# A decoder layer on one core: one more reserved k-block at the product boundaries, turned blocks in two PSUM banks, a longer written order and a shorter norm chain

## The chip, the cores and the metric

The kernel runs on one core of a Trainium2 chip. The core has a matrix engine (TensorE, "PE" in the profile, with its weight loads as "PEld"), a vector engine (VectorE, "DVE"), a scalar engine (ScalarE, "ACT"), GpSimd ("POOL"), SyncE ("SP", which here issues the loads) and 16 DMA engines. Each engine works through its own queue of instructions in order and waits for the others by semaphores. SBUF holds operands, and PSUM holds what TensorE accumulates: here eight banks of 128 x 512 fp32. The metric is device time in microseconds (us), the median of the runs.

## The reference: one decoder layer in fp32

The input x is 256 tokens of 2048 numbers. A vector c gives, through a matrix w_ada, nine vectors of 2048 (three shifts, three scales, three gates):

```python
mod = (c_act @ w_ada[l] + b_ada[l]).reshape(b, N_MOD, D_MODEL)
h = modulate(rms_norm(x, norm_ffn1[l]), mod[:, 0], mod[:, 1])
x = x + 0.5 * mod[:, 2][:, None, :] * swiglu(h, w_ffn1_gu[l], w_ffn1_down[l])
h = modulate(rms_norm(x, norm_mix[l]), mod[:, 3], mod[:, 4])
x = x + mod[:, 5][:, None, :] * token_mixing(h, w_in[l], w_ret_branch[l], w_swa_branch[l], w_out[l], sinks[l])
h = modulate(rms_norm(x, norm_ffn2[l]), mod[:, 6], mod[:, 7])
x = x + 0.5 * mod[:, 8][:, None, :] * swiglu(h, w_ffn2_gu[l], w_ffn2_down[l])
return rms_norm(x, norm_final)
```

`swiglu(h, w_gu, w_down)` splits `h @ w_gu` into a gate and an up half of 5632 columns each and returns `(silu(gate) * up) @ w_down`. `token_mixing` is one product with `w_in`, a retention and a sliding-window attention, and a product with `w_out`. `rms_norm` divides a token's row by the root of the mean of its squares (plus 1e-6); `modulate` is `h * (1 + scale) + shift`. Three times, then, a product ends that writes into x (here called the down product: 5632 to 2048, 2048 to 2048, 5632 to 2048), a norm over the whole row of x follows, and twice the next product starts from the normed row. These places are the boundaries.

## The kernel before

**Products.** The 256 tokens are two halves t = 0, 1 of 128. An fp32 product is made of three products in a reduced format, fp32r: each operand is split into a high part (ACT's cast) and the rest (DVE's subtraction), and `products()` (L342 to L344) issues high x high, low x high and high x low for each half and each 128 rows of the sum ("k-tile"). A weight chunk is 512 rows (one "k-block") by 512 columns, loaded by SP into one of four `raw` buffers; it is split in two half-blocks of 256 rows (cast `wh` L350, subtraction `wl` L352), with three buffers each for high and low. A half-block for both halves of the tokens is 12 matmuls. Activations that lie in a `slot` are split in pairs (`Whole.pair`, L385 and L386) into two "a" buffers; those of a normed row are kept whole, split, in `Held` ("hh", "hl").

**PSUM.** Four banks accumulate products ("pa"), two hold turned blocks ("ps"), and two ("pd") serve for smaller things, the unread output of the squares among them.

**Order.** A scheduler orders PE, DVE and ACT freely, with one exception each for a down product's end and the norm behind it, which stand inside `manual_schedule(engines=ORDERED)` and so in the order in which the code is written. SP is always in written order. In `down_product`, two column chunks (0 and 1) come first, with free order. Of the second pair of chunks (2 and 3), the last three k-blocks are reserved: chunk 2 is computed there for both halves, chunk 3 is only split, into buffers that are kept (`late`, `home`), and then computed half by half: `last(0, steps)` for t = 0 in one go, and for t = 1 in six steps of six matmuls, handed on as `tail`. In this way the first half's row of x is complete while TensorE still has six steps to do. `add_gated` (L571, L572) multiplies a bank with the gate and adds it to x, and ACT sums the squares (L487).

**The norm and the next product's head** (`into_norm`). `inv_rms` (L499 to L513) adds the four chunks' squares, takes a root on ACT and a reciprocal with one Newton step on DVE. Of each half, four blocks of 512 columns are then scaled (`normed`, L533), turned by four transposes into one PSUM bank (`turned`, L540), scaled and shifted by columns (`modulated4`: the first two, once three, columns on ACT, L552, and the others on DVE, L554) and split into `Held` (`to_held`, L563 and L564). The first chunk of the next product (its "head", two banks) is computed as the blocks come. The first boundary leads from the first feed-forward's down product to `w_in`, the second from `w_out` to the second feed-forward, and the third to the output (`final`, from L1220).

**The conditioning.** The nine vectors are worked out on DVE beside the products, paced by `set_pace` and `tick` over a given number of half-blocks.

## Time and profile before

| | |
|---|---|
| median of 3 runs | 2422.79 us (2422.41 to 2423.88) |
| the profiled execution | 2424.86 us |
| its span, from first to last instruction | 2423.1 us |
| granted TensorE clock | 0.999 |
| busy: PE, PEld | 2376.9 us (98%), 1936.8 us (80%) |
| busy: DVE, ACT, POOL | 1700.1 us (70%), 1290.0 us (53%), 5.6 us (0%) |
| read from HBM | 595.06 MB, 246 GB/s over the span |

A row of a timeline gives the start in us from the span's start, the duration, engine, line, operation, out<-in by the program's names, shape, how many stand in a row, and in brackets the idle time ahead and whose work ended it. A row of busy windows gives the stretch and its length, then busy us and count of PE, PEld, DVE, ACT and POOL, then granted clock, DMA share and GB/s. A row of groups gives line, engine, operation, shapes and count, then busy us and mean ns of one, then the idle time ahead and whom it waited for. A row of waits gives who waits for whom, the idle time in us, how often, and the longest. The first boundary lies at about 742 to 802 us of the span, the second at about 1653 to 1713, the last reserved section at about 2383 to 2393 with the output behind it.

### The profile page before, as it was taken

Reading aid. Unit: us, or ns where it says so; the run is one execution under the profiler, and the core shown is the slowest. Engines: PE = TensorE matmul, PEld = TensorE weight load, DVE = VectorE, ACT = ScalarE, POOL = GpSimd, SP = SyncE. Lnnn points to the kernel's source line nnn. Section 1 sums busy time; section 2 is a strip of 40 time slices with the busy share of each in tenths; the row PEclk is TensorE's granted clock in tenths of the full one; section 3 lists DMA queues with packets and bytes.
Section 4 is the critical chain, followed back from the end, with each engine's and each line's share of the span. In section 5 each row is a group of like instructions: output and inputs, shape, how many; then the busy total and the mean of one; then the engine's idle time right before and its main releaser. Section 6 shows DMA issues by size and latency. Waiting matters only on the chain. (4 is left out here: it accounts for less than half of the span.)

```text
span 2423.1 us, 28959 instructions
## 1 busy us (share of the span) xinstructions
PE 2376.9 (98%) x10678; PEld 1936.8 (80%) x10678; DVE 1700.1 (70%) x2736; ACT 1290.0 (53%) x1789; POOL 5.6 (0%) x14
## 2 busy tenths in 40 slices
PE   7999999999999999999999999999999999999998
PEld 4778888888787787778888788887888888888886
DVE  6998887778877668876766776767655555545656
ACT  6544544454545456665555554455555545454544
POOL 0000000000000000000000000000000000000000
PEclk9999999999999999999999999999999999999999
DMA  9997689998875697766679887765677887875563
GB/s 351 337 333 286 215 312 307 372 311 307 302 270 191 243 270 224 226 232 213 212 257 288 252 281 263 278 199 183 224 245 234 244 253 242 257 225 191 185 200 122
DMA packets 307184, 614.29 MB, mean 254 GB/s; under 512 B 72737, under 2 KB 73121, under 8 KB 288225
## 3 DMA queue, kind: packets, MB, share of 16 engines
q1 hardware_dynamic: 305538, 605.78, 75.0%
q0 software_dynamic: 928, 5.61, 0.7%
q8 instruction: 84, 1.38, 0.2%
q10 hardware_dynamic: 576, 1.05, 0.1%
q14 instruction: 58, 0.48, 0.1%
HBM read 595.06 MB, written 2.12 MB: 246 GB/s over the span
## 5 line engine op out<-in xcount | busy, mean ns | idle before, releaser
L352 DVE TENSOR_TENSOR wl<-raw,wh 128x1024 fp32r<-128x1024 f32 (+1 forms) x828 | 994.0, 1208 | 557.1 <-ACT wh L350 552.3
L350 ACT CAST wh<-raw 128x1024 fp32r<-128x1024 f32 (+1 forms) x828 | 859.7, 1041 | 960.7 <-PE pa L343 940.4
L342 PE MATMUL pa<-wh,hh 128*128 128x512 f32 x2224 | 870.3, 392 | 3.4 <-ACT wh L350 2.8
L343 PE MATMUL pa<-wh,hl 128*128 128x512 f32 x2224 | 869.0, 391 | 2.2 <-DVE hl L528 1.8
L344 PE MATMUL pa<-wl,hh 128*128 128x512 f32 x2224 | 796.7, 392 | 4.1 <-DVE wl L352 3.7
L344 PEld LDWEIGHTS pa<-wl,hh 128*128 128x128 f32 x2224 | 415.1, 188 | 97.4 <-DVE wl L352 10.4
L342 PEld LDWEIGHTS pa<-wh,hh 128*128 128x128 f32 x2224 | 418.1, 188 | 93.4 <-ACT wh L350 4.2
L343 PEld LDWEIGHTS pa<-wh,hl 128*128 128x128 f32 x2224 | 418.3, 188 | 91.8 <-issue 3.0
L343 PE MATMUL pa<-wh,a 128*128 128x512 f32 x992 | 384.0, 389 | 1.4 <-DVE a L386 1.4
L344 PE MATMUL pa<-wl,a 128*128 128x512 f32 x992 | 366.7, 390 | 2.2 <-DVE wl L352 2.2
L342 PE MATMUL pa<-wh,a 128*128 128x512 f32 x992 | 367.3, 390 | 1.2 <-DVE t L571 1.2
L344 PEld LDWEIGHTS pa<-wl,a 128*128 128x128 f32 x992 | 185.9, 188 | 42.7 <-DVE wl L352 4.5
L342 PEld LDWEIGHTS pa<-wh,a 128*128 128x128 f32 x992 | 186.1, 188 | 41.2 <-DVE t L571 1.9
L343 PEld LDWEIGHTS pa<-wh,a 128*128 128x128 f32 x992 | 186.2, 188 | 40.5 <-DVE a L386 2.2
L206 DVE CUSTOM_DVE_ANT_0 slot<-slot,cact 128x512 f32<-128x512 f32 (+1 forms) x252 | 193.0, 815 | 30.2 <-DMA slot<-in_w_ada_dram 30.0
L206 DVE CUSTOM_DVE_ANT_0 raw<-raw,cact 128x512 f32<-128x512 f32 (+1 forms) x260 | 167.3, 696 | 49.3 <-DMA raw<-in_w_ada_dram 39.1
L386 DVE TENSOR_TENSOR a<-slot,a 128x512 fp32r<-128x512 f32 x124 | 84.9, 685 | 13.6 <-ACT a L385 13.6
L385 ACT CAST a<-slot 128x512 fp32r<-128x512 f32 x124 | 76.4, 618 | 14.8 <-PE pa L344 14.7
L467 ACT COPY slot<-back 128x512 uint16<-128x512 uint16 x116 | 77.2, 767 | 0.0
L453 ACT COPY flat<-t 128x512 uint16<-128x512 uint16 x104 | 59.1, 619 | 4.1 <-DVE t L1097 3.8
L206 DVE DVE_READ_ACCUMULATOR2_ANT sums<- 128x1 f32 x512 | 42.4, 83 | 0.0
L487 ACT ACTIVATE pd<-x_sb 128x512 f32<-128x512 f32 x32 | 19.0, 593 | 34.8 <-DVE x_sb L572 32.5
(166 smaller groups left out, 990.2 us busy)
## 6 DMA issues: line engine op xcount, KB each, us to landing
raw<-in_w_ffn_gu_dram SPq DMA_DIRECT2D x152, 1024.0 KB, 5.5
raw<-in_w_in_dram SPq DMA_DIRECT2D x104, 1024.0 KB, 5.3
raw<-in_w_ffn_down_dram SPq DMA_DIRECT2D x88, 1024.0 KB, 5.2
slot<-in_w_ada_dram SPq DMA_DIRECT2D x76, 1024.0 KB, 7.5
raw<-in_w_ada_dram SPq DMA_DIRECT2D x64, 1024.0 KB, 5.2
raw<-in_w_ffn_gu_dram SPq DMA_DIRECT2D x24, 768.0 KB, 6.9
raw<-in_w_swa_branch_dram SPq DMA_DIRECT2D x16, 1024.0 KB, 5.6
raw<-in_w_ret_branch_dram SPq DMA_DIRECT2D x16, 1024.0 KB, 5.2
```

The lines of the kernel that those rows point to most:

```text
L206: nc.vector.tensor_tensor_reduce(out=w[:, at], in0=w[:, at], in1=cact[:, at], scale=1.0, scalar=0.0, op0=ALU.mult, op1=ALU.add, accum_out= ...
L342: nc.tensor.matmul(ps, ah[:, j, ts], wh[:, j, :], start=first, stop=False)
L343: nc.tensor.matmul(ps, al[:, j, ts], wh[:, j, :], start=False, stop=False)
L344: nc.tensor.matmul(ps, ah[:, j, ts], wl[:, j, :], start=False, stop=last)
L350: cast.append(nc.scalar.copy(hi, src).ins)
L352: nc.vector.tensor_sub(lo, src, hi.bitcast(F32))
L385: nc.scalar.copy(hi, v)
L386: nc.vector.tensor_sub(lo, v, hi.bitcast(F32))
L453: nc.scalar.copy(planes[:, i, :], words(src)[:, :, i])
L467: nc.scalar.copy(into[:, :, :, i], held["turned"][:, i])
L487: nc.scalar.activation(side_bank(), src, AF.Square, accum_out=dest)
```

## The change

Seven edits, all at the boundaries and the norms:

1. The last four instead of the last three k-blocks are reserved, so `tail` has eight steps of six matmuls. The first of the four keeps its activation pairs in buffers of its own ("back"), and its weights of chunk 3 in the half of the next `Held` that is not yet written (`spare_of`; at the program's end in a tile of the freed "hl").
2. A turned block lies in two banks: ACT's columns in "ps", DVE's in "pd". `ON_ACT` says how many columns are ACT's (2 or 3 of 4).
3. The order is written as a list of words. A digit pair is the half and the block: n norm, t transposes, ma and md the columns of ACT and DVE, h and l the split, p six matmuls of the head (half, k-block, half-block); tail0 to tail7 are six matmuls each; w10a and w10d the high and low part of half-block 0 of the head's weight 1; mul, add, sq the gated addition in pieces; rs, v, q, r the norm chain.
4. The list ends with the first weights of the product that follows the head (x0a to x1d), handed on as `ahead`; their load stands with the head's.
5. The norm chain: squares of three chunks are added beforehand (`mean_of_three`), and when the fourth is there, ACT takes `Abs_reciprocal_sqrt` and DVE makes the Newton step in two operations beside one that is independent of the root; the factor -1/2 that this leaves goes into the scalings (`HALF`), and where there is none, into one more small multiplication at the kernel's start.
6. The unread output of the last square goes to an SBUF tile ("flat") and the normed blocks too.
7. The first conditioning stretch is paced over 150 instead of 154 half-blocks.

```diff
-    def gemm_part(act, w, col0s, banks, kb, KT):
+    def gemm_part(act, w, col0s, banks, kb, KT, ahead=None):
...
-            raw = load(w, kb, c0)
+            raw = None if ahead else load(w, kb, c0)
...
-                wh, wl = split(wsp, "w", raw[:, 2 * h : 2 * h + 2, :], CH)
+                if ahead:
+                    wh, wl = ahead[h]
+                else:
+                    wh, wl = split(wsp, "w", raw[:, 2 * h : 2 * h + 2, :], CH)
...
+    def weight_by_parts(w, kb, c0, home=None):
+        raw = load(w, kb, c0)
+        made = {}
+        def high(h):
+            if home is None:
+                made[h] = [
+                    wsp.tile([P, 2, CH], F32R, tag=tag, name=nm(tag)) for tag in ("wh", "wl")
+                ]
+            else:
+                views = home()
+                made[h] = [view[:, 2 * h : 2 * h + 2, :] for view in views]
+            nc.scalar.copy(made[h][0], raw[:, 2 * h : 2 * h + 2, :])
+        def low(h):
+            hi, lo = made[h]
+            pace["behind"] = nc.vector.tensor_sub(
+                lo, raw[:, 2 * h : 2 * h + 2, :], hi.bitcast(F32)
+            )
+        return high, low, made
...
-    def square_sum(dest, src):
-        nc.scalar.activation(side_bank(), src, AF.Square, accum_out=dest)
+    def flat_tile():
+
...
-        nc.scalar.activation(r, s, AF.Sqrt, bias=eps, scale=1.0 / D)
...
+    HALF = -0.5
+    class Root:
+        def __init__(self, ssq, t):
+            self.base = mean_of_three(ssq, t)
+            self.last = ssq[:, t * 4 + 3 : t * 4 + 4]
+            self.r, self.v, self.q = (small(1, tag) for tag in ("rs1", "var", "rq1"))
+        def root(self):
+            nc.scalar.activation(
+                self.r, self.last, AF.Abs_reciprocal_sqrt, bias=self.base, scale=1.0 / D
+            )
+        def mean(self):
+            nc.vector.tensor_scalar(
+                out=self.v, in0=self.last, scalar1=1.0 / D, scalar2=self.base,
+                op0=ALU.mult, op1=ALU.add,
+            )
+        def near(self):
+            nc.vector.scalar_tensor_tensor(
+                out=self.q, in0=self.v, scalar=self.r, in1=self.r, op0=ALU.mult, op1=ALU.mult
+            )
+        def nearer(self):
+            nc.vector.scalar_tensor_tensor(
+                out=self.r, in0=self.q, scalar=-3.0, in1=self.r, op0=ALU.add, op1=ALU.mult
+            )
...
-        for kb in range(nb - 3):
+        for kb in range(nb - 4):
...
+            def place(kb, h):
+                if kb >= a:
+                    halves = home[:, (kb - a) * 2 + h].rearrange("p (i n) -> p i n", i=2)
+                    return [halves[:, i] for i in range(2)]
+                if kb == a - 1:
+                    return None
+                return [back.tile([P, CH], F32R, tag="back", name=nm("back")) for _ in range(2)]
+            for kb in (a - 2, a - 1, a, b):
...
-                n = kb + 1 if kb < b else a - 1
-                wt = weight(w, n, c0s[1], None if n < a else home_tile())
+                n = {a - 2: a - 2, a - 1: a, a: b, b: a - 1}[kb]
+                wt = weight(
+                    w, n, c0s[1], spare if n == a - 2 else None if n < a else home_views()
+                )
                 late[n] = [(n, h, wt(h)) for h in range(2)]
-            steps = [step for kb in (a - 1, a, b) for step in late[kb]]
+            steps = [step for kb in (a - 2, a, a - 1, b) for step in late[kb]]
...
+            def gated(t):
+                y[t] = t512()
+                nc.vector.tensor_mul(y[t], banks[1][t], gate[:, c0 : c0 + CH])
+            def added(t):
+                xs = x_sb[:, t, c0 : c0 + CH]
+                nc.vector.tensor_add(xs, xs, y[t])
+            def squared(t):
+                square_sum(
+                    ssq[:, t * 4 + 3 : t * 4 + 4], x_sb[:, t, c0 : c0 + CH], flat_tile
+                )
             after(
-                ssq,
-                lambda t: add_gated(banks[1][t], t, c0s[1], gate, ssq),
-                [lambda i=i: last(1, steps[i : i + 1]) for i in range(6)],
-            )
...
+    ORDER = """
+            w10a tail0 mul0 add0 tail1 sq0 rs0 v0 tail2 q0 r0 n00 n02 t00 tail3 md00
+            ma00 n03 h00 tail4 n01 w20a l00 t02 w21a w20d tail5 ma02 md02 w10d t01 tail6
+            h02 w21d w11a p000 ma01 l02 md01 tail7 w11d h01 t03 w30a mul1 p020 l01 w31a
...
+    ON_ACT = (2, 3, 3, 3, 2, 3, 3, 3)
...
+            wide = {"w1": weight_by_parts(w, 1, c0)}
+            wide["w2"] = weight_by_parts(w, 2, c0, at_first_use(home_views))
+            wide["w3"] = weight_by_parts(w, 3, c0, at_first_use(home_views))
+            wide["x"] = weight_by_parts(w, 0, c1)
+            xn, hs, ps = {}, {}, {}
+            def norm(t, kb):
+                xn[t, kb] = flat_tile()
+                xs = x_sb[:, t, kb * CH : (kb + 1) * CH]
+                nc.vector.tensor_scalar(
+                    out=xn[t, kb], in0=xs, scalar1=roots[t].r, scalar2=HALF,
+                    op0=ALU.mult, op1=ALU.mult,
+                )
+            def turn(t, kb):
+                ps[t, kb] = bank(), side_bank()
+                for j in range(KB):
+                    js = slice(j * P, (j + 1) * P)
+                    to = ps[t, kb][j >= ON_ACT[t * 4 + kb]]
+                    nc.tensor.transpose(to[:, js], xn[t, kb][:, js], ident)
...
+            def high(t, kb):
+                h4, hi, _ = of_held(t, kb)
+                nc.scalar.copy(hi, h4)
+            def low(t, kb):
+                h4, hi, lo = of_held(t, kb)
+                nc.vector.tensor_sub(lo, h4, hi.bitcast(F32))
...
+            for word in ORDER:
+                name = word.rstrip("0123456789")
+                if word[0] in "wx":
+                    of, h, low_part = word[:-2], int(word[-2]), word[-1] == "d"
+                    wide[of][low_part](h)
+                    if low_part and of != "x":
+                        parts[int(of[1]), h] = wide[of][2][h]
+                elif name in whole:
+                    whole[name](int(word[len(name) :]))
+                else:
+                    block[name](*map(int, word[len(name) :]))
+            ahead.update(wide["x"][2])
...
-    set_pace([(2, None, 0.5), (4, 1, None), (3, None, None)], 154, place, AQ)
+    set_pace([(2, None, 0.5), (4, 1, None), (3, None, None)], 150, place, AQ)
...
-    held, head, *calls = into_norm(3, wi, O_SK)
-    down_product(Whole(tiles), dn, gate, KF, *calls)
+    held, head, ahead, *calls = into_norm(3, wi, O_SK, O_SV)
+    down_product(Whole(tiles), dn, gate, KF, spare_of(held), *calls)
...
-    b = in_chunk(O_SV)
+    b = gemm(held, wi, [O_SV], ahead=ahead)[0]
```

How this moves instructions, at three places of DVE's queue. The first is the first boundary, from the first half's first scaling (out is the scaled block, `rs` the root) over the columns (`modc` scale and shift) and the splits (`hl`, `wl`, `home` are low parts), before:

```order
L533 TENSOR_SCALAR t_5920<-x_sb,rs_1048_5911 128x512 [waits DVE_49]
L533 TENSOR_SCALAR t_5922<-x_sb,rs_1048_5911 128x512
L352 TENSOR_TENSOR wl_5965<-raw_5896,wh_5964 128x1024 [waits PE_49,Activation_49]
L554 TENSOR_SCALAR t_5968<-ps_5948,modc 128x128 [waits PE_49,Activation_49]
L554 TENSOR_SCALAR t_5968<-ps_5948,modc 128x128
L564 TENSOR_TENSOR hl_4137<-t_5968,hh_4136 128x4x128 [waits Activation_49]
L533 TENSOR_SCALAR t_5975<-x_sb,rs_1048_5911 128x512
L533 TENSOR_SCALAR t_5977<-x_sb,rs_1048_5911 128x512
L554 TENSOR_SCALAR t_5979<-ps_5959,modc 128x128 [waits PE_49,Activation_49]
L571 TENSOR_TENSOR t_5995<-pa_5057,row_2516 128x512 [waits PE_49]
```

and with the change:

```order
L791 TENSOR_SCALAR flat_5932<-x_sb,rs_1039_5885 128x512 [waits DVE_49]
L791 TENSOR_SCALAR flat_5934<-x_sb,rs_1039_5885 128x512
L819 TENSOR_SCALAR t_5948<-pd_5937,modc 128x128 [waits PE_49]
L819 TENSOR_SCALAR t_5948<-pd_5937,modc 128x128
L791 TENSOR_SCALAR flat_5953<-x_sb,rs_1039_5885 128x512
L791 TENSOR_SCALAR flat_5962<-x_sb,rs_1039_5885 128x512 [waits DVE_49]
L835 TENSOR_TENSOR hl_4141<-t_5948,hh_4140 128x4x128 [waits Activation_49]
L467 TENSOR_TENSOR home_5964<-raw_5896,home_5964 128x1024 [waits DMAHW7_49,Activation_49]
L819 TENSOR_SCALAR t_5981<-pd_5968,modc 128x128 [waits PE_49]
L467 TENSOR_TENSOR wl_5903<-raw_5894,wh_5902 128x1024 [waits DMAHW6_49]
```

The columns' rows (L554, now L819) named a wait for PE and ACT and now name PE alone, from a "pd" bank; the weights' subtractions (L467) stand further back among the blocks.

The second place is the second boundary's down product, the first reserved k-block of chunks 2 and 3 with the gated additions of chunks 0 and 1 (`row` is the gate, `raw` the weight, `slot` the activations), before:

```order
L352 TENSOR_TENSOR wl_12922<-raw_12919,wh_12921 128x1024
L386 TENSOR_TENSOR a_12913<-slot_10598,a_12913 128x512
L571 TENSOR_TENSOR t_12889<-pa_12579,row_10597 128x512
L571 TENSOR_TENSOR t_12894<-pa_12580,row_10597 128x512
L352 TENSOR_TENSOR wl_12938<-raw_12919,wh_12937 128x1024
L572 TENSOR_TENSOR x_sb<-x_sb,t_12889 128x512
L572 TENSOR_TENSOR x_sb<-x_sb,t_12894 128x512
```

and with the change:

```order
L385 TENSOR_TENSOR back_12937<-slot_10596,back_12936 128x512
L603 TENSOR_TENSOR t_12887<-pa_12577,row_10595 128x512
L603 TENSOR_TENSOR t_12892<-pa_12578,row_10595 128x512
L352 TENSOR_TENSOR wl_12941<-raw_12914,wh_12940 128x1024
L604 TENSOR_TENSOR x_sb<-x_sb,t_12887 128x512
L604 TENSOR_TENSOR x_sb<-x_sb,t_12892 128x512
L445 TENSOR_TENSOR hl_12575<-raw_12956,hh_12574 128x1024
L603 TENSOR_TENSOR t_12897<-pa_12579,row_10595 128x512
L603 TENSOR_TENSOR t_12902<-pa_12580,row_10595 128x512
L445 TENSOR_TENSOR hl_12575<-raw_12956,hh_12574 128x1024
L385 TENSOR_TENSOR a_12964<-slot_10596,a_12964 128x512
L352 TENSOR_TENSOR wl_12968<-raw_12962,wh_12967 128x1024
```

The additions begin at the same place, ahead of `wl_12941`, the k-block's second weight; the two subtractions into `hl` (chunk 3's weight of this k-block) come among them, and six of the eight half additions (L603, L604) precede `wl_12968`, the next k-block's first weight.

The third place is the program's end, from the last gated multiplication to the last root, before:

```order
L571 TENSOR_TENSOR t_18442<-pa_17583,row_13494 128x512
L572 TENSOR_TENSOR x_sb<-x_sb,t_18442 128x512
L1226 TENSOR_TENSOR t_18438<-x_sb,gf 128x512
L499 TENSOR_REDUCE sum_18448<-ssq_16737 128x1
L503 TENSOR_SCALAR var_18449<-sum_18448 128x1
L506 RECIPROCAL rs_3273_18450<-rs_3273_18450 128x1
L507 SCALAR_TENSOR_TENSOR rq_3274_18451<-var_18449,rs_3273_18450 128x1
L510 TENSOR_SCALAR rq_3274_18451<-rq_3274_18451 128x1
L513 TENSOR_TENSOR rs_3273_18450<-rs_3273_18450,rq_3274_18451 128x1
```

and with the change:

```order
L739 TENSOR_TENSOR t_18442<-pa_17580,row_13500 128x512
L743 TENSOR_TENSOR x_sb<-x_sb,t_18442 128x512
L1313 TENSOR_TENSOR t_18438<-x_sb,gf 128x512
L565 TENSOR_SCALAR var_18360<-ssq_16734,base_18356 128x1
L571 SCALAR_TENSOR_TENSOR rq_3260_18361<-var_18360,rs_3258_18359 128x1
L576 SCALAR_TENSOR_TENSOR rs_3258_18359<-rq_3260_18361,rs_3258_18359 128x1
```

Six operations between the last addition and the scaling have become three.

More of the change, by code (lines that the diff above doesn't have):

```diff
@@ L664, in down_product @@
                 for h in range(2):
[L665 to L668 removed]
+                    pairs[kb].append(act.pair(kb * 2 + h, place(kb, h)))
                     products(
@@ L784, in layer_kernel @@
+        return held, banks, ahead, before, after
     gu, dn = w_ffn1_gu[0], w_ffn1_down[0]
@@ L844, in layer_kernel @@
             )
-    r = [inv_rms(ssq, t) for t in range(NT)]
+    r = [Root(ssq, t).all() for t in range(NT)]
+    for t in range(NT):
+        nc.vector.tensor_scalar(out=r[t], in0=r[t], scalar1=HALF, scalar2=None, op0=ALU.mult)
     bounds = (0, 2, 5, 8, 12, 16)
@@ L1234, in final @@
             scaled(3)
-            r = inv_rms(ssq, t)
+            r = roots[t].all()
             for ci in range(4):
```

253 lines of the change are left out of this document (109 added, 144 removed).

## The prediction

> **What bounds the kernel now.** I read the page's busy times first, then TensorE's matmuls in the timeline, then its busy time around the three reserved stretches, then who it waited for there.
>
> ```profile
> PE 2376.9 (98%) x10678; PEld 1936.8 (80%) x10678; DVE 1700.1 (70%) x2736; ACT 1290.0 (53%) x1789; POOL 5.6 (0%) x14
> ...
> 745.31 0.51 PE L344 MATMUL pa<-wl,home 128*128 128x512 f32 x1 [0.64 <-DVE wl L352]
> 746.12 0.39 PE L344 MATMUL pa<-wl,home 128*128 128x512 f32 x1
> 750.66 0.39 PE L343 MATMUL pa<-wh,home 128*128 128x512 f32 x1
> ...
> 742.00:802.00 60.00, 55.06 (x246) 42.32 (x245) 46.74 (x82) 34.30 (x58) 0.53 (x1) 1.00 0.53 182
> 1653.00:1713.00 60.00, 56.00 (x251) 43.46 (x250) 46.27 (x79) 35.85 (x60) 0.00 (x0) 1.00 0.48 164
> 2383.00:2393.00 10.00, 9.29 (x38) 6.78 (x37) 10.00 (x12) 8.64 (x11) 0.00 (x0) 1.00 0.59 210
> ...
> 742.00:802.00 60.00, 4.88 (x32) 3.82 (x32) 1.00 0.53 182
> ```
>
> TensorE is the bound and works almost always, so a time can only come out of what it loses. From 746.12 to 750.66 stand 20 matmuls: 0.227 us each when nothing is missing, though each shows 0.39 (they overlap). Busy time therefore hides losses, and I count matmuls. The windows give span, then PE, PEld, DVE and ACT busy with counts; the last row is the transposes alone (L540, 32 of them, 8 groups of 4).
>
> First boundary: 246 - 32 = 214 wide matmuls x 0.227 = 48.6 us. A group of transposes takes 0.44 us undisturbed (769.83 to the next matmul below, 0.35, plus 0.09 of restart): 3.5 us. 60.0 - 48.6 - 3.5 = 7.9; the count takes in the matmuls cut at both ends, so up to 0.4 more. I take 8.2 us. Second: 219 x 0.227 = 49.7, so 6.8 to 7.2; I take 7.1. Last reserved section: 10.0 - 38 x 0.227 = 1.4 to 1.8; I take 1.6. **16.9 us** in all is lost around these stretches; that is the most the change can win on TensorE there. Who is waited for, at the first one (idle alone, without restarts):
>
> ```profile
> PE ps L540 <- DVE t L533: 1.4, 2, 1.0
> PE pa L344 <- DVE wl L352: 1.3, 3, 0.6
> PE pa L342 <- ACT wh L350: 1.2, 1, 1.2
> PE pa L342 <- ACT hh L563: 0.5, 1, 0.5
> PE pa L343 <- DVE hl L564: 0.5, 2, 0.2
> ```
>
> Two kinds, then: the turned blocks and splits of the handover, and at the section's start the split weights (745.31 above). The handover in detail, from the end of the last product's first half:
>
> ```profile
> 764.58 0.69 DVE L571 TENSOR_TENSOR t<-pa,row 128x512 f32<-128x512 f32 x1 [0.93 <-PE pa L344]
> 766.63 0.19 ACT L487 ACTIVATION_READ_ACCUMULATOR pd<-x_sb 128x1 f32 x1
> 766.85 0.16 DVE L499 TENSOR_REDUCE sum<-ssq 128x1 f32<-128x4 f32 x1 [0.85 <-ACT pd L487]
> 767.04 0.30 ACT L502 ACTIVATE rs<-sum,eps 128x1 f32<-128x1 f32 x1 [0.22 <-DVE sum L499]
> 767.57 0.22 DVE L507 SCALAR_TENSOR_TENSOR rq<-var,rs 128x1 f32<-128x1 f32 x1
> 768.21 0.88 DVE L533 TENSOR_SCALAR t<-x_sb,rs 128x512 f32<-128x512 f32 x2
> 769.83 0.60 PE L540 MATMUL ps<-small_c,t 128*128 128x128 f32 x4
> 770.46 0.81 ACT L552 ACTIVATE t<-ps,modc 128x128 f32<-128x128 f32 x2 [2.19 <-PE ps L540]
> 771.30 0.73 DVE L554 TENSOR_SCALAR t<-ps,modc 128x128 f32<-128x128 f32 x2 [1.08 <-ACT t L552]
> 772.12 0.62 ACT L563 CAST hh<-t 128x512 fp32r<-128x512 f32 x1 [0.85 <-DVE t L554]
> 772.78 0.69 DVE L564 TENSOR_TENSOR hl<-t,hh 128x512 fp32r<-128x512 f32 x1 [0.74 <-ACT hh L563]
> ...
> 780.45 0.66 PE L540 MATMUL ps<-small_c,t 128*128 128x128 f32 x4 [1.04 <-DVE t L533]
> 782.33 0.60 PE L540 MATMUL ps<-small_c,t 128*128 128x128 f32 x4
> 783.48 0.49 PE L342 MATMUL pa<-home,hh 128*128 128x512 f32 x1 [0.54 <-ACT hh L563]
> 784.20 0.50 PE L343 MATMUL pa<-home,hl 128*128 128x512 f32 x1 [0.23 <-DVE hl L564]
> ```
>
> A block is a strict chain: transposes, ACT's two columns, DVE's two, cast, subtraction. From 780.45 to its first product at 783.48 are 3.0 us, to the low part at 784.20 3.75; between them the program has six matmuls (1.36) and one other group (0.44). TensorE waits for the rest.
>
> **The handover, cost 0 after the change (-6.7 and -5.6 us).** These are 8.2 and 7.1 without the section starts, 1.5 each (below). The cover is the written list: a "tail" or "p" word is six matmuls, 1.36 us; a "t" 0.44.
>
> Norm: before, 766.82 (end of the read) to 768.21, 1.39 us. Now the sum of three chunks is ready earlier, and what follows the last square is root (0.30 and a gap, 0.33), L571 (0.26 with its gap) and L576 (0.26): 0.85, so 0.54 less. From the product's end (764.54) the first norm then ends at 768.70 - 0.54 = 768.16, 3.6 us; tail0 to tail2 cover 4.1 less the 0.16 that the last matmul runs over its pace. Slack 0.3.
>
> Blocks: of after, the chain is shorter by the two DVE columns behind ACT's (0.73), longer by a third ACT column (0.36): 2.6 us to the high part, 3.3 to the low one. Covers between a "t" and its first "p": t00 6.3 (tail3 to tail6, t02, t01), t02 6.3, t01 and t03 7.2, t10 3.6 (p001, p030, t12, t11), t12 3.2 (t11, p100, p101), t11 5.9, t13 4.1. The low part is needed one matmul (0.23) later, so t12 is short by 0.0 and the others have spare. Throughput: from the first norm DVE has 8 norms x 0.44, 10 columns x 0.37, 8 subtractions x 0.61, 8 weight subtractions x 1.14 and 2.5 for the second half's addition and norm: 23.7 us; TensorE has 5 tails, 8 groups and 16 words p: 32.1 us. DVE is not the bound, ACT with the 20 us of its casts and 22 columns neither.
>
> The work moved: the DVE subtractions and ACT casts of the next product's first weights (2 x 1.14) now lie inside that 23.7; their load moves ahead on SP, past the first conditioning load, and takes the fourth raw buffer; the 1.2 us "PE wh L350" wait that today follows the handover goes with it. Otherwise SP's order shifts only where the conditioning's loads go by the new pace, and POOL's not at all.
>
> DVE's columns carry a wait for TensorE alone now, where today they wait for TensorE and ACT (the first place shown with the change). Today's 1.08 us at 771.30 is a wait for ACT, and by that row it could be for the bank or for the result tile that both write. The Trainium skill, "PSUM — Partial Sum Buffer", section "PSUM bank collisions raise a hardware error", says that two engines must not touch one bank at once, two readers included, while different banks run clean; here that would make the bank the cause, and the new banks its cure. Were it the tile, each block would keep 0.7 us, and only t10 and t12 would show it, some 1 us in both boundaries together: -14 instead of -15.
>
> **The reserved sections.** DVE needs per k-block 4 weight and 2 activation subtractions, TensorE 24 matmuls = 5.44 us:
>
> ```profile
> L352 DVE TENSOR_TENSOR wl<-raw,wh 128x1024 fp32r<-128x1024 f32 x15 | 18.1, 1222 | 3.4 <-ACT wh L350 3.4
> L386 DVE TENSOR_TENSOR home<-slot,home 128x512 fp32r<-128x512 f32 x4 | 2.7, 684 | 0.0
> ...
> 738.42 0.62 ACT L385 CAST a<-slot 128x512 fp32r<-128x512 f32 x1 [3.41 <-PE pa L344]
> 741.17 2.35 DVE L427 TENSOR_TENSOR home<-raw,home 128x1024 fp32r<-128x1024 f32 x2
> ...
> 1633.43 1.05 ACT L350 CAST wh<-raw 128x1024 fp32r<-128x1024 f32 x1 [2.12 <-PE pa L343]
> 1636.26 1.28 DVE L571 TENSOR_TENSOR t<-pa,row 128x512 f32<-128x512 f32 x2
> ```
>
> Back to back a weight takes 1.14 (two in 2.35, less the overhang) and an activation 0.60: 5.75 per block, 0.3 more than TensorE. So a section costs little if DVE enters it ahead, and the 3.41 us in which ACT waited at 738.42 for an "a" buffer are the lead lost today. The first of the four blocks gets buffers of its own, so that wait falls out. Lead: ACT fills three weight buffers; when TensorE frees one, two half-blocks (2 x 2.72) are in stock, less cast 0.95 and subtraction 1.14: 3.3 us. Up to the next block's first weight DVE has 5 x 1.14 + 2 x 0.60 = 6.9 against 5.44 + 3.3: no wait. First and last section: -1.5 and -1.6 (at worst, with no lead, they keep 1.5 plus 0.3 for each of three blocks).
>
> Second boundary: its product has only four k-blocks, so all are reserved, and the four gated additions of the first column half stand inside the first ones, where the scheduler could not spread them. In DVE's order there (the second place shown with the change) six of the eight half additions (0.60 each) come before the next block's weight: 6.9 + 3.6 = 10.5, against 5.44 + 3.3: late by 1.8, plus 0.3 for restart and 0.3 each in the two blocks that follow. It replaces today's 1.5 there: **-1.5 + 2.5**. Ends: 0 (longer lead) and 6.0 (none).
>
> **The end.**
>
> ```profile
> 2413.22 0.39 PE L344 MATMUL pa<-home,home 128*128 128x512 f32 x1
> 2415.63 0.19 ACT L487 ACTIVATION_READ_ACCUMULATOR pd<-x_sb 128x1 f32 x1
> 2417.21 1.28 DVE L1238 TENSOR_SCALAR t<-t,rs 128x512 f32<-128x512 f32 x3
> ```
>
> The same norm chain, exposed: 1.39 becomes 0.85. **-0.5**.
>
> **Prices the trace lacks.** The new root function: 0.30 by L502, at most 0.8 as a gated column pair (L552); nearest is L502, three times on the path: 0 to +1. Norms with a second constant: 0.44 by L533 or 0.69 by a two-tensor L571; sixteen, hidden but for the first (+0.25, inside its slack). The unread square output in SBUF: 0.62, as ACT's cast, for 0.60. One more 128x1 multiplication at the kernel's start, 0.16 by L499, against the shorter chain: 0. Conditioning in 150 instead of 154 half-blocks: DVE's same work 3% denser, 30% of it idle: 0, give or take 1.
>
> **Sum.** -6.7 -5.6 (handovers) -1.5 -1.6 (sections) -1.5 +2.5 (second section) -0.5 = **-14.9 us**. The profiled execution took 2424.86 us (span 2423.1 and 1.8 around it), so 2410.0 there; the median shown is 2422.79, 2.1 lower, so **2408**.
>
> **Rivals.**
> - DVE late in all sections (for it: 5.75 against 5.44; against it: the private buffers). Without any lead: second section 6.0, the others 2.4 each, 8.3 more than the sum: 2416.
> - Each block is waited for: the list gives the engines no run-ahead, because an in-order queue stops at an early word (mul1 on DVE waits for tail7, and l01 stands behind it). Then 16 blocks pay w each. At w = 0.93 nothing is won, above 1.23 the kernel is slower by over 0.2%; with no cover at all w = 3.2 - 0.44, 44 us: 2452. Against it: the covers of 3.2 to 7.2 us.
> - The change moves the wait only: TensorE gets through the handovers, but the next product's weights and conditioning, which today are done in those gaps, come as much later. For it: DVE is busy 46.7 of 60 us there; against: that leaves 13 idle. Some 2422.
>
> **Chances.** Forecast 0.78; late sections 0.12; waited-for blocks 0.06, some of it above w = 1.23; moved only 0.04. I call 0.2% (4.8 us) what a measurement tells from nothing. Faster: 0.78 + 0.12 = 0.90; same 0.05, slower 0.05. The range runs from all of 16.9, the end and a quiet conditioning (2404) to the late sections (2416.5).
>
> **What would show it.** Right: no idle before the transposes and before the products on the held pairs in both handovers, DVE's columns starting with ACT's, a wait of 2 to 3 us for "wl" near the start of the second reserved section and none in the other two, 0.85 us from the last read to the last scaling. Wrong: any of these waits at a block's first product, or TensorE waiting for weights after the handover.

## The result, and the profile after

The changed kernel takes 2407.54 us (median of 6 runs, 2406.89 to 2411.14), the kernel before 2422.44 us beside it (6 runs, 2422.15 to 2423.88): 14.9 us less, a ratio of 0.9939 with a 95% interval of 0.9929 to 0.9950. The profiled execution took 2406.89 us with a span of 2404.9.

The page's busy times of the changed kernel, and its busy windows, counted as in the prediction: the first handover, the second reserved section, the second handover, the last section; the last two rows are the transposes alone (now L801).

```profile
PE 2369.5 (99%) x10678; PEld 1937.5 (81%) x10678; DVE 1694.8 (70%) x2720; ACT 1293.9 (54%) x1799; POOL 5.7 (0%) x14
...
730.00:790.00 60.00, 60.00 (x282) 49.74 (x281) 42.97 (x67) 37.47 (x64) 0.53 (x1) 1.00 0.60 209
1625.00:1650.00 25.00, 23.65 (x99) 18.08 (x98) 24.34 (x28) 19.65 (x29) 0.00 (x0) 1.00 0.78 264
1650.00:1710.00 60.00, 60.00 (x281) 49.72 (x280) 40.51 (x75) 34.39 (x60) 0.00 (x0) 1.00 0.45 163
2360.00:2380.00 20.00, 20.00 (x90) 16.53 (x90) 16.33 (x23) 11.15 (x15) 0.00 (x0) 1.00 0.25 92
...
730.00:790.00 60.00, 4.63 (x32) 3.91 (x32) 1.00 0.60 209
1650.00:1710.00 60.00, 4.63 (x32) 3.91 (x32) 1.00 0.45 163
```

In the first handover stand 250 wide matmuls at 0.227 us and eight groups of transposes at 0.44: 56.8 + 3.5 fill the 60 us. Nothing is lost where 6.7 us were. In the second, 249 of them and the transposes fill them too. The last section has 90 in 20.0 us, without loss. Only the second reserved section still loses: 25.0 less 99 x 0.227 is 2.5 us, and up to 2.8 by the matmuls' starts. The view of what TensorE waits for there names one thing, the split weights (idle alone; each wait costs 0.3 to 0.6 us more in restarts):

```profile
PE pa L344 <- DVE wl L352: 1.3, 2, 0.6
...
1633.08 0.50 PE L344 MATMUL pa<-wl,a 128*128 128x512 f32 x1 [0.64 <-DVE wl L352]
1640.03 0.50 PE L344 MATMUL pa<-wl,home 128*128 128x512 f32 x1 [0.63 <-DVE wl L352]
```

The timeline of the first block, from the last step of the norm chain to its low part:

```profile
762.02 0.16 DVE L576 SCALAR_TENSOR_TENSOR rs<-rq,rs 128x1 f32<-128x1 f32 x1
762.22 0.88 DVE L791 TENSOR_SCALAR flat<-x_sb,rs 128x512 f32<-128x512 f32 x2
763.12 0.38 PE L801 MATMUL ps<-small_c,flat 128*128 128x128 f32 x2
763.33 0.38 PE L801 MATMUL pd<-small_c,flat 128*128 128x128 f32 x2
763.53 0.81 ACT L815 ACTIVATE t<-ps,modc 128x128 f32<-128x128 f32 x2 [1.80 <-PE ps L801]
763.75 0.73 DVE L819 TENSOR_SCALAR t<-pd,modc 128x128 f32<-128x128 f32 x2 [0.65 <-PE pd L801]
764.57 0.62 ACT L831 CAST hh<-t 128x512 fp32r<-128x512 f32 x1 [0.23 <-DVE t L819]
765.22 0.69 DVE L835 TENSOR_TENSOR hl<-t,hh 128x512 fp32r<-128x512 f32 x1
```

The transposes have no wait ahead of them, DVE's columns start 0.22 us after ACT's instead of behind them, and the high part is ready 2.1 us after the first transpose, the low one 2.8.

The end, from the last read of the squares to the last scalings:

```profile
2397.82 0.19 ACT L532 ACTIVATION_READ_ACCUMULATOR flat<-x_sb 128x1 f32 x1
...
2398.62 0.16 DVE L576 SCALAR_TENSOR_TENSOR rs<-rq,rs 128x1 f32<-128x1 f32 x1
2398.81 0.72 ACT L1336 ACTIVATE t<-t,rs 128x512 f32<-128x512 f32 x1 [0.48 <-DVE rs L576]
```

All these programs have 10678 matmuls, so traces can be laid beside each other by the matmul's number. The table gives the time between the starts of two matmuls, in us, for two profiled executions of each kernel (the second ones are the first two experiments below):

```
matmul                        before        changed       difference
200 to 2800                592.41 591.49  592.04 592.15   within the spread
2800 to 3400, section and
  first handover           140.67 140.66  132.53 132.53     -8.1
3400 to 7000               771.09 767.82  768.12 767.82      0.0
7000 to 7400, section       91.43  91.43   92.56  92.54     +1.1
7400 to 7600, handover      47.11  47.11   41.87  41.87     -5.2
7600 to 10400              633.69 633.68  633.71 633.71      0.0
10400 to 10600, section     46.99  46.97   45.33  45.33     -1.6
last matmul to the end       9.88   9.87    9.54   9.53     -0.3
```

At the five places two executions agree within 0.02 us, and their differences, before rounding, sum to -14.2. Cut at matmul 3200, which in both kernels lies behind the section and ahead of the first transposes, the first place gives the section alone, 92.3 us before and 90.7 now (-1.65), and the handover alone, 48.3 and 41.9 (-6.5). The first 200 matmuls, the start-up, end between 71.8 and 73.7 us in the traces of this study.

### The profile page after: what moved, and what is told of

Same layout as the page of the kernel before. It is cut to its first block, busy times and chain, and to the rows that moved or that the text cites. A ratio compares the mean times of both kernels' runs of the same rounds, so it can differ in the third digit from the quotient of the medians.

```text
span 2404.9 us, 28941 instructions
## 1 busy us (share of the span) xinstructions
PE 2369.5 (99%) x10678; PEld 1937.5 (81%) x10678; DVE 1694.8 (70%) x2720; ACT 1293.9 (54%) x1799; POOL 5.7 (0%) x14
## 5 line engine op out<-in xcount | busy, mean ns | idle before, releaser
L352 DVE TENSOR_TENSOR wl<-raw,wh 128x1024 fp32r<-128x1024 f32 (+1 forms) x806 | 968.2, 1207 | 560.4 <-ACT wh L350 555.6
L350 ACT CAST wh<-raw 128x1024 fp32r<-128x1024 f32 (+1 forms) x806 | 837.3, 1041 | 950.4 <-PE pa L343 932.7
L342 PE MATMUL pa<-wh,hh 128*128 128x512 f32 x2192 | 856.3, 392 | 2.3 <-ACT wh L350 1.8
L343 PE MATMUL pa<-wh,hl 128*128 128x512 f32 x2192 | 855.9, 391 | 2.1 <-DVE hl L597 2.1
L344 PE MATMUL pa<-wl,hh 128*128 128x512 f32 x2192 | 784.3, 392 | 2.5 <-DVE wl L352 2.4
L343 PE MATMUL pa<-wh,a 128*128 128x512 f32 x944 | 365.1, 389 | 0.0
L342 PE MATMUL pa<-wh,a 128*128 128x512 f32 x944 | 350.0, 391 | 1.1 <-ACT wh L350 0.5
L344 PE MATMUL pa<-wl,a 128*128 128x512 f32 x944 | 349.0, 390 | 1.5 <-DVE wl L352 1.4
L344 PEld LDWEIGHTS pa<-wl,a 128*128 128x128 f32 x944 | 177.0, 188 | 40.2 <-DVE wl L352 3.5
L342 PEld LDWEIGHTS pa<-wh,a 128*128 128x128 f32 x944 | 177.1, 188 | 39.7 <-DVE slot L1277 1.0
L343 PEld LDWEIGHTS pa<-wh,a 128*128 128x128 f32 x944 | 177.1, 188 | 36.6 <-DVE a L385 0.2
L968 DVE TENSOR_TENSOR slot<-slot,pa 128x512 f32<-128x512 f32 x56 | 35.8, 681 | 0.0
```

The costliest lines, as they stand in the source:

```text
L342: nc.tensor.matmul(ps, ah[:, j, ts], wh[:, j, :], start=first, stop=False)
L343: nc.tensor.matmul(ps, al[:, j, ts], wh[:, j, :], start=False, stop=False)
L344: nc.tensor.matmul(ps, ah[:, j, ts], wl[:, j, :], start=False, stop=last)
L350: cast.append(nc.scalar.copy(hi, src).ins)
L352: nc.vector.tensor_sub(lo, src, hi.bitcast(F32))
L968: nc.vector.tensor_add(p, p, b)
```

## The experiments

Each kernel was timed beside the kernel before on the same chip. Where a small difference counts, the trace decides; the five places of the table above, in each kernel:

```
                             2800-3400  7000-7400  7400-7600  10400-10600   end
kernel before                  140.66      91.43      47.11      46.97      9.87
  two banks                    138.54      91.43      45.05      46.97      9.87
  shorter norm chain           140.05      91.43      46.55      47.01      9.30
changed kernel                 132.53      92.54      41.87      45.33      9.53
  one bank                     132.53      92.55      41.87      45.33      9.28
  tails first                  136.68      92.54      46.03      45.33      9.53
  tails first, one bank        139.91      92.54      49.31      45.33      9.30
  pairs' buffers exchanged     134.50      93.27      41.87      47.28      9.32
  old norm chain               132.82      92.58      42.20      45.33      9.88
  first weights not ahead      132.53      92.54      41.87      45.33      9.29
  additions put off            132.53      89.79      41.87      45.33      9.32
```

### The kernel before, again

No edit.

> The kernel before, unchanged, in one more profiled execution. The two profiled executions differ by 18.0 us (2424.86 and 2406.89), the medians by 14.9. Theory: about 2.4 us of it are two waits of TensorE at 1351 and 1367 us of the first profile, behind a conditioning load that landed late in that one execution; here they are absent and the span is 2420.5 to 2421. Rival: they belong to the program and the change took them away; then they stand here too and the span is 2423.

Measured: 2421.46 us, span 2419.6. The two waits are gone, and TensorE waits for nothing between 1340 and 1370 us. DVE there, in the first profile and then in this one:

```profile
1346.84 0.69 DVE L206 CUSTOM_DVE_ANT_0 raw<-raw,cact 128x512 f32<-128x512 f32 x1 [3.05 <-DMA raw<-in_w_ada_dram]
```

```profile
1344.16 0.69 DVE L206 CUSTOM_DVE_ANT_0 raw<-raw,cact 128x512 f32<-128x512 f32 x1 [0.43 <-DMA raw<-in_w_ada_dram]
```

A conditioning load landed 2.6 us later in the first profile, and what DVE had queued behind it came late for TensorE. It belongs to that execution, not to the program: the sum of the prediction is rightly held against 14.9 us and not against the 18.0 between the two profiled executions.

### The changed kernel, again

No edit.

> The changed kernel, unchanged, beside the next one on one chip. It should take 2407.5 us, and 14.9 us less than the kernel before; its waits in the second reserved section (2.6 us) stand as in the first profile.

Measured: 2407.76 us (5 runs) beside 2422.51, ratio 0.9939 (0.9926 to 0.9951). The waits of the second section stand as before, 1.3 us in two.

### One bank per block, the list kept

```diff
-                ps[t, kb] = bank(), side_bank()
+                ps[t, kb] = [bank()] * 2
```

> The changed kernel with each turned block in one PSUM bank again; everything else, the order too, is kept. Theory of the prediction (the written list covers the chain, only t10 and t12 are short): the column that is written later waits for the other engine, 0.4 to 0.7 us per block, and the time grows by about 1 us, to 2408.5. Rival (the second bank carries the gain): each of 16 blocks pays up to 0.73 us, 11.7 us, 2419. In the trace: idle of TensorE ahead of the products on held pairs.

Measured: 2407.41 us, no difference, and no step at either boundary in the trace. The wait itself is back, here in the second block:

```profile
769.14 1.15 ACT L815 ACTIVATE t<-ps,modc 128x128 f32<-128x128 f32 x3
770.32 0.41 DVE L819 TENSOR_SCALAR t<-ps,modc 128x128 f32<-128x128 f32 x1 [0.78 <-ACT t L815]
```

The tile that both write is the same as in the changed kernel; only the bank differs. So the bank is the cause of the wait, and the list covers it everywhere, in t12 by little (its transposes, with t11's; the first product behind both; its low part):

```profile
783.12 1.03 PE L801 MATMUL ps<-small_c,flat 128*128 128x128 f32 x8
...
783.91 0.48 PE L342 MATMUL pa<-home,hh 128*128 128x512 f32 x1
...
786.05 0.69 DVE L835 TENSOR_TENSOR hl<-t,hh 128x512 fp32r<-128x512 f32 x1 [0.69 <-ACT hh L831]
```

The low part ends at 786.74, 3.6 us after the first transpose. Twelve matmuls of p100 and p101 (2.7 us from 783.91) and one more stand before the matmul that needs it. In the trace that one starts at 786.97, 0.23 us later, and its weight load at 786.74, in the moment in which the low part is ready: nothing is to spare.

### Two banks in the kernel before

The blocks' transposes go to "ps" and "pd" by columns; order, chain and reserved steps stay as before.

```diff
     def turned(xn, on_act):
-        ps = psum()
+        ps = bank(), side_bank()
...
-            nc.tensor.transpose(ps[:, js], xn[:, js], ident)
+            nc.tensor.transpose(ps[j >= on_act][:, js], xn[:, js], ident)
```

> The kernel before with only the turned blocks put into two PSUM banks, its order and chain kept. If the bank is why DVE's columns wait for ACT, the 1.08 us wait at the first block's DVE columns goes, each block is shorter by up to 0.73 us, and three waits of 0.6 to 1.2 us per boundary shrink by as much: 3 to 4 us in both boundaries, 2419. If the result tile is the cause, the wait stays and the time is 2422.4. Either way most of the 14.9 us stays with the order.

Measured: 2416.96 us beside 2421.28, ratio 0.9982 (0.9972 to 0.9991), 4.3 us; the matmuls come 2.1 us earlier over each handover. DVE's columns at the first block:

```profile
770.37 0.73 DVE L554 TENSOR_SCALAR t<-pd,modc 128x128 f32<-128x128 f32 x2 [0.24 <-PE pd L540]
```

The wait of 1.08 us for ACT has become one of 0.24 us for TensorE. What is worth 4.2 us alone is worth nothing beside the list: the parts of this change do not add up, they cover the same waits. The Trainium skill, "PSUM — Partial Sum Buffer", section "PSUM bank collisions raise a hardware error", says that two engines must be kept from touching one bank at once and that different banks run clean; the trace agrees in that the wait follows the bank, at this place 1.08 us for ACT with one and 0.24 for TensorE with two.

### The tails ahead of the first transposes

```diff
-            ... n00 n02 t00 tail3 md00
-            ma00 n03 h00 tail4 n01 w20a l00 t02 w21a w20d tail5 ma02 md02 w10d t01 tail6
-            h02 w21d w11a p000 ma01 l02 md01 tail7 w11d ...
+            ... n00 n02 tail3 tail4 tail5 tail6 tail7 t00 md00
+            ma00 n03 h00 n01 w20a l00 t02 w21a w20d ma02 md02 w10d t01
+            h02 w21d w11a p000 ma01 l02 md01 w11d ...
```

> The changed kernel with tail3 to tail7 moved ahead of the first transposes in TensorE's order, so that five steps of six matmuls, 6.8 us, no longer lie between the turned blocks; all else in the list is kept. Theory (these steps are the cover): the first block has 0.9 us of cover for 2.6 us, 1.7 us of wait, and DVE's columns and splits of the first four blocks come later in the same way: 3.4 us at the least, 13.6 us at the most in both boundaries, 2411 to 2421. Rival (the gain comes from the banks and the shorter chain, the cover is not needed): under 1 us.

Measured: 2417.92 us, 10 us above the changed kernel; by the trace 4.15 us in the first boundary and 4.16 in the second, 8.3 us. What TensorE waits for in the first:

```profile
PE pa L343 <- DVE hl L835: 1.3, 1, 1.3
PE ps L801 <- DVE flat L791: 1.3, 1, 1.3
PE ps L801 <- ACT t L815: 0.8, 1, 0.8
```

The same instructions with the same durations: only the cover between a block's transposes and its products is gone, and more than half of what the handovers won goes with it. The waits stand at several steps of the blocks' chain, not at the first product alone. The medians lie 2 us further apart than the traces say. The profiled execution is the shortest of ten, with a granted clock of 0.999; six of the others took 2417.4 to 2419.6 us at 0.997, and the remaining three 2416.4 to 2417.1 at 0.998 or 0.999. A lower clock in those six fits the 2 us; where it fell in them no trace shows.

### The tails first, and one bank

Both edits above.

> The kernel with the tails ahead of the first transposes, and one PSUM bank per turned block as well. One bank cost nothing where the list covers the chain, and the kernel before won 4.2 us by two. Theory (the bank costs only where a block's chain is not covered): one to two blocks per boundary pay 0.7 us each, 1.5 to 3 us in all above the kernel with the tails first, 2419.5 to 2421. Rival (with the columns' new order the bank costs nothing anywhere): 2417.9.

Measured: 2422.88 us, 5.0 us more than with the tails first alone, 3.2 and 3.3 us in the boundaries by the trace. So the bank costs as soon as the chain is bare, and all gain is lost. It costs more than the 1.5 to 3 us that I worked out; two lines of TensorE's timeline and the busy windows of this kernel show why (the column behind POOL is the granted clock):

```profile
777.09 0.66 PE L801 MATMUL ps<-small_c,flat 128*128 128x128 f32 x4 [1.24 <-DVE t L819]
...
779.96 0.79 PE L343 MATMUL pa<-home,hl 128*128 128x512 f32 x1 [1.72 <-DVE hl L835]
...
773.00:780.00 7.00, 3.78 (x16) 2.11 (x16) 5.29 (x7) 6.19 (x11) 0.00 (x0) 0.98 0.00 1
780.00:783.00 3.00, 3.00 (x7) 2.42 (x8) 3.00 (x5) 2.51 (x3) 0.53 (x1) 0.50 0.87 289
783.00:786.00 3.00, 3.00 (x14) 2.39 (x14) 2.35 (x7) 2.74 (x8) 0.00 (x0) 0.98 0.96 354
```

After two waits of 1.24 and 1.72 us close together the granted clock was 0.50 for 3 us: seven matmuls at 0.43 instead of 0.227 us, 1.4 us. Without it the boundary pays 1.8 us. By the matmuls' starts this comes from three waits that are longer than with two banks, by some 0.8, 0.5 and 0.4 us. By the traces the bank costs 6.5 us in both boundaries, 2.8 of it by the clock; the medians differ by less, 5.0, which fits the lower clock in six of the runs with the tails first alone.

### The pairs' buffers exchanged

```diff
-                if kb == a - 1:
+                if kb == a - 2:
                     return None
```

> The changed kernel with the buffers of the first two reserved k-blocks' activation pairs exchanged: the first takes the two shared a buffers, the second the private ones. Theory (the wait for an a buffer is what costs DVE its lead at a section's start): ACT waits some 3 us for an a buffer at each section's start again and TensorE pays about 1.5 us there in all three sections, 4.6 us in all, 2412. Rival (the lead does not hang on these buffers): no change, 2407.5.

Measured: 2412.66 us, 5.1 us above the changed kernel. By the trace the first section pays 2.0 us, the second 0.7, the last 1.9: 4.6. ACT's and TensorE's waits at the first section:

```profile
ACT a L384 <- PE pa L344: 5.8, 2, 3.4
```

```profile
PE pa L344 <- DVE wl L352: 0.6, 1, 0.6
```

ACT's wait is that of the kernel before, "3.41" us in its longest, and TensorE's wait for "wl" is back. The lead does hang on these buffers. The two whole sections pay 0.4 us more than the 1.5 I gave them, in the main since one more k-block is late in each: by the matmuls' starts the first late one costs 1.3 us and two behind it 0.24 to 0.28 each, as "0.3 more than TensorE" per block said, and in the kernel before, with one reserved k-block fewer, only one follows; in the second section the gated additions make DVE late either way, and the buffers add only 0.7.

### The old norm chain

The sum of four, the square root, the reciprocal and the Newton step in three operations, with the factor in the scalings set to 1; the order kept.

```diff
         def root(self):
+            nc.vector.tensor_reduce(out=self.s, in_=self.all_four, axis=AX.X, op=ALU.add)
-            nc.scalar.activation(
-                self.r, self.last, AF.Abs_reciprocal_sqrt, bias=self.base, scale=1.0 / D
-            )
+            nc.scalar.activation(self.r, self.s, AF.Sqrt, bias=eps, scale=1.0 / D)
...
-    HALF = -0.5
+    HALF = 1.0
```

> The changed kernel with the old norm chain (sum of four, square root, reciprocal, Newton step in three operations, no factor in the scalings); the order is kept. Theory: the chain is 0.54 us longer; all of it shows at the program's end, and in the two handovers what goes beyond the slack of 0.3 us, 0.24 each ahead of the first transposes: 1.0 us in all, 2408.5. Rival: it is on the path in every place, 1.6 us; or only at the end, 0.5 us.

Measured: 2409.84 us, 2.1 to 2.3 us above the changed kernel. The trace gives 0.3 us more in each handover, with a wait ahead of the first transposes where there was none, and 9.88 us from the last matmul to the end instead of 9.53. TensorE's waits at the first boundary:

```profile
PE ps L803 <- DVE flat L793: 0.2, 1, 0.2
```

A chain that is 0.54 us longer costs 0.3: the slack is 0.24 us, for which I had 0.3. These places hold 1.0 us, as worked out. The rest is not at them; 1.0 us lies between matmul 200 and 2800 of this one execution, where the other traces spread from 591.2 to 593.0, and that it has to do with the chain is not shown.

### The shorter norm chain in the kernel before

The class of the change put into the kernel before, with its root and factor; order, banks and steps stay.

```diff
-            r = inv_rms(ssq, 0)
+            r = roots[0].all()
...
-            r = inv_rms(ssq, 1)
+            r = roots[1].all()
```

> The kernel before with only the shorter norm chain. Theory: 0.54 us less at the program's end, and as much at the second half's norm in each of the two handovers, where TensorE waited 1.0 us for the scaled block: 1.6 us in all, 2420.8. Rival: in the handovers another step of the chain is late instead, 0.5 us.

Measured: 2419.81 us beside 2422.51, ratio 0.9989 (0.9980 to 0.9998). That is 2.7 us less, with an interval of 0.5 to 4.8. By the trace 0.6 us in each handover and 0.57 at the end, 1.7 us; the other 1.0 is not found at these places. TensorE's wait for the scaled blocks at the first boundary, 1.4 us before:

```profile
PE ps L566 <- DVE t L557: 0.8, 2, 0.5
```

### The next product's first weights left to that product

```diff
-            wide["x"] = weight_by_parts(w, 0, c1)
...
-            ahead.update(wide["x"][2])
```

The four words x0a to x1d are left out of the list as well.

> The changed kernel without the first weights of the product behind the head in the written list; they are loaded and split by that product itself again. Theory: TensorE waits for them behind the handover as before (there 2.6 us of loss at 794 to 800 us of the first boundary and 1.4 us at 1705 to 1709 of the second), 1.2 us at the least and 4.0 us at the most, 2409 to 2411.5. Rival (a scheduler that is free again takes them ahead anyway): no change, 2407.5.

Measured: 2407.87 us, no difference; TensorE waits for nothing between 725 and 805 us. The rival holds. Where the list keeps DVE and ACT ahead, the scheduler brings these splits in time by itself. That the waits at 794 to 800 us in the kernel before came from engines that left the handover late is my reading, not a test of its own; it fits that there ACT does three of these casts in a row from 795.68, right behind its last block's (in its second trace).

### The second boundary's additions put off

Where all k-blocks are reserved, the second chunk's multiplications stand ahead of the last kept weight, and the four additions behind the last split.

```diff
+        gate_old(0)
+        if nb > 4:
+            gate_old(1)
+            add_old()
...
+                if kb == b and nb == 4:
+                    gate_old(1)
+                    banks[1] = [acc_bank() for _ in range(NT)]
...
+            if nb == 4:
+                add_old()
             last(0, steps)
```

Here `gate_old` multiplies a finished chunk with the gate into two tiles, and `add_old` adds all four to x and sums the squares.

> The changed kernel with the gated additions of the second boundary's first two column chunks put off where all its k-blocks are reserved: the multiplications of the second chunk ahead of the last kept weight, the four additions behind the last split. Theory (six half additions ahead of the next k-block's weight make the waits at 1632 to 1646 us): these waits go, 2.6 us less, 2405. Rival: the waits have another cause (the section starts without lead, or a load), and nothing is won, 2407.5; or the put-off multiplications are late for the second chunk's bank, and TensorE waits there, up to 2 us more.

Measured: 2404.29 us (5 runs, 2403.68 to 2405.03) beside 2422.22, ratio 0.9927 (0.9915 to 0.9940). Since the gain is small, it was run once more beside the changed kernel:

> The changed kernel with the gated additions put off, again, beside the changed kernel. The first run gave 3.2 us less and its trace lost 2.8 us of waits. Theory: 2.8 us less than the changed kernel of the same job. Rival: the difference was one between jobs, under 1 us.

Measured: 2404.01 us against 2407.76, and 2422.51 for the kernel before (ratio 0.9926, 0.9913 to 0.9938). The medians differ by 3.75 us. The two profiled executions, which differ by 4.3, show where: the second section's matmuls come 2.75 us earlier, 1.2 lie in the start-up, which this edit does not touch, and the rest is spread. So 2.75 us are shown to be the edit's. The section's window, with 112 matmuls where 99 stood:

```profile
1625.00:1650.00 25.00, 25.00 (x112) 20.70 (x111) 24.70 (x28) 18.30 (x25) 0.00 (x0) 1.00 0.86 305
```

This version beats both kernels.

## Why the prediction was right, point by point

- **The total.** 2408 was forecast, 2407.54 measured; the sum of -14.9 stands against -14.2 at the five places and -14.9 between the medians. That the medians meet it to the tenth is luck: 0.7 us of them lie outside the five places, where two executions of one kernel differ by as much.
- **The handovers, "cost 0 after the change".** Forecast -6.7 and -5.6, measured -6.5 (the first place's -8.1 without the section's -1.65) and -5.2. That the list is the cover is shown by the tails moved first, 8.3 us back with every duration kept.
- **The norm, "Slack 0.3".** 0.24 by the old chain. From the end of the last read (2398.01) to the scalings (2398.81) are 0.8 us, 0.85 forecast.
- **Blocks.** 2.1 us to the high part and 2.8 to the low one for a block with two columns on ACT, against the forecast of 2.6 and 3.3 for three. The chain was right, the cover too small: I counted it from the block's last transpose and the chain from its first, so the 0.4 us of a block's own transposes are missing in every cover. The size of the chain held: in t12, with three columns on ACT, 2.5 and 3.2 us. t12, "short by 0.0", has 0.4 us to the weight load that needs its low part and 0.6 to the matmul, and t10 more, and the one-bank term, "some 1 us in both boundaries together", measured 0.0. This is the term that was mis-sized.
- **The two banks.** I weighed the bank as part of what makes the handovers cost nothing. The wait does follow the bank, but in the changed kernel the bank moves the time by nothing; it is worth 4.2 us in the old order, and where the cover is taken away 5.0 us by the medians (6.5 by the traces, 2.8 of it the lower clock).
- **"The work moved".** I wrote that the 1.2 us wait for the next product's first weights goes because they are split ahead. It goes without that: with the list in place the step has no effect of its own.
- **The sections.** First -1.5 and last -1.6, measured -1.65 each; the private buffers are the reason (without them 2.0 and 1.9 us come back there). The second, "-1.5 + 2.5", came to +1.1, and 2.75 us go when the additions are put off, so the cause was right. The terms behind the 2.5 (1.8, 0.3 for a restart, 0.3 in each of two blocks) add up to 2.7. Their shape was not as worked out: not one wait of 1.8 us at the second reserved k-block, but two of 0.6 us of idle, at the second (1633.08, where the matmuls' starts lose 0.9 us) and at the third (1640.03, 1.25), and 0.2 us behind each; the last two half additions stand on DVE between the two waits (1633.55).
- **The end.** -0.5 forecast, -0.3 to -0.6 in the traces of the changed kernel and its variants.
- **The conditioning at 150 half-blocks, "0, give or take 1".** Matmuls 200 to 2800, where it runs, take 592.0 and 592.2 us against 591.5 and 592.4: nothing beyond what two executions differ by. It was not undone by itself, and neither were the fourth reserved k-block (only its buffers were) and the SBUF tiles of the sixth edit.

The rivals: sections late without lead and blocks waited for did not happen, and the buffers exchanged and the tails first show what each would have cost. "Moved only" falls with the zeros between the places.

## What to carry to other kernels

At a handover between products, count for each result the matmuls that the written order puts between its making and its use, and compare that with its chain: where the cover is longer, a faster chain, a second bank or an earlier load brings nothing, and where it is shorter each of them brings time, at most its own size. Parts of such a change overlap, so each has to be undone and done alone before a gain is put down to it. And where a stretch is computed in a written order, look for work that the order has pushed into its first blocks: putting off six half additions was worth 2.75 us without a faster instruction.

## What the runs showed of the hardware that I had not expected

TensorE's clock fell to 0.50 for 3 us after two waits of 1.24 and 1.72 us within 4.1 us (tails first and one bank; 3.78 us busy of 7.00), so that the waits cost 1.4 us more than their length. It did so at both boundaries. With the tails first and two banks the longest wait was 1.3 us, and in the profiled execution the granted clock of the same stretch stayed at 1.00:

```profile
773.00:780.00 7.00, 4.84 (x22) 3.49 (x23) 6.75 (x9) 6.76 (x12) 0.00 (x0) 1.00 0.19 43
780.00:783.00 3.00, 3.00 (x14) 2.46 (x14) 2.38 (x7) 2.61 (x7) 0.53 (x1) 1.00 0.97 388
```

The Trainium skill, "TensorE: Matmul & The Clock Gate", section "Part 1: The HAM clock gate (the "warmup" mystery)", gives in its table of the two states an idle window of about 3.4 us as what halves the clock; here shorter waits were enough, with some matmuls between them, and the measurement decides. How much shorter they can be is not shown: six of the ten runs with the tails first and two banks had a mean clock of 0.997, as the runs with one bank did (0.995 to 0.997), and none of the six was traced.
